# Column sums taken tile by tile, inverses nine slots behind, all constants at the start: an RWKV kernel on one core

## The chip, the cores and the metric

One core of a Trainium2 chip. The metric is the device time of one execution in microseconds (us), smaller is better; each version was run several times and its median is given. Ratios are computed as the mean time of one kernel's fast runs over that of the other's fast runs of the same rounds, so they are not quite the ratio of the medians quoted beside them. A run counts as "slow" when it is over 1.5% above the fastest of the same kernel.

## The reference, cut to what matters

```python
# k, v: (16, 2048, 256) float32; w, u: (256,)
for b in range(batch):
    aa = bb = 0; pp = -1e38                    # one state per channel
    for t in range(seq_len):
        kk, vv = k[b, t], v[b, t]
        qq = maximum(pp, u + kk); e1 = exp(pp - qq); e2 = exp(u + kk - qq)
        output[b, t] = (e1 * aa + e2 * vv) / (e1 * bb + e2 + 1e-08)
        qq = maximum(pp - w + kk, kk)           # [cut: as written]
        aa, bb, pp = e1 * aa + e2 * vv, e1 * bb + e2, qq
```

The kernel turns the loop over time into prefix sums. A tile holds 128 time steps of 4 batches (128 x 1024 values); there are 64 tiles, and four tiles (16 batches) share the same stretch of time. Between stretches, a state goes from one to the next.

## The kernel before

PE is TensorE (the matrix products), DVE VectorE, ACT ScalarE, POOL GpSimd; SP issues the small transfers. PE writes its products to PSUM, which the kernel divides into eight banks. Each turn of the loop, called a slot, brings one tile in and takes an older one out; `LAG` is how many slots behind the inverse of the denominators follows. `EZR` is a ring of twelve tiles: quarters 0 and 1 hold exponentials, quarters 2 and 3 the same times `v`.

```python
for n in range(NP + LAG + 2):                   # NP = 64, LAG = 10
    q, qp = n - LAG, n - LAG - 1
    num(qp, NUMB, 0)                            # PE: numerators, first half, into the one bank NUMB
    den(q)                                      # PE: denominators
    small_work(n, "nums")
    exps(n)                                     # ACT: exponentials of the new tile
    small_work(n, "act")
    recip(q)                                    # ACT: 1/den as Ln, then Exp
    mult(qp, NUMB, 0)                           # DVE: output, first half
    small_work(n, "mid")
    round_k(n + 2)                              # DVE: k to fp32r
    num(qp, NUMB, 1); mult(qp, NUMB, 1); store(qp)
    small_work(n, "chain")
    times_v(n)                                  # DVE: exponentials times v
    cast_v(n + 1); logs(n + 1)                  # DVE: v to bf16; PE: exponents of the next tile
    small_work(n, "pe"); small_work(n, "last")
    # [cut: the conditions for the first and last slots]
```

Once in four slots (a period) the state is worked on, spread over slots by the list `plan`. It is turned so that channels lie on partitions, worked on, turned back by PE, copied to `cb` by DVE, and sent into the tiles by four small transfers:

```python
def sums(c):                                    # PE: 32 matmuls, column sums of a period's four tiles
    ...
def inject(c):                                  # the state goes back into row 63 and 127 of four tiles
    cb = small.tile([128, 128], BF16, tag="cb", name="cb")
    K(DVE.tensor_copy(cb, st.pop((c, "CT"))))
    r0 = 4 * c % RING
    for q in range(2):                          # q = 0: the quarters that num reads; q = 1: those of den
        for h in range(2):
            r, x = HS * h + HS - 1, 32 * (2 * q + h)
            K(SP.dma_start(out=EZR[r:r + 1, 2 * (1 - q), ...], in_=cb[x:x + 32, :]))   # [cut]

plan = [(s + 1, "pe", sums), (s + 2, "mid", copy_sums), (s + 2, "pe", turn),
        (s + 3, "act", state_logs), (s + 3, "chain", state_offsets),
        (s + 4, "act", state_weights), (s + 4, "chain", state_chain),
        (s + 5, "nums", turn_back), (s + 5, "mid", inject)]      # s = 4c + 3
```

## Time and profile before

| | us |
|---|---|
| time, median of 3 runs | 331.42 (331.21 to 332.84) |
| span of the profiled run | 328.2 |
| start, to the end of the twelfth product (slot 12 begins) | 56.96 |
| middle, from there to the beginning of slot 63 | 231.66 |
| drain, from there to the end | 39.62 |

A period below is the mean of ten, slots 16 to 55. The three stages have different bounds, which is why the page's shares (PE 81%, DVE 85%, ACT 78%) decide nothing by themselves. The prediction below shows the lines: the loads and the half clock in the start, DVE in the middle, ACT's Ln and Exp pairs in the drain.

### The profile page before, as it was taken

To read this page: it belongs to the slowest core of one execution; us is meant where nothing else is said; L and a number is where in the kernel's file an instruction comes from. 1 tells how busy PE (TensorE), PEld (TensorE's weight loads), DVE (VectorE), ACT (ScalarE), POOL (GpSimd) and SP (SyncE) were. 2 spreads that over 40 slices of the span, in tenths; PEclk is the share of its full clock that TensorE was granted. 3 is DMA by queue.
4 is the path that set the end of the run, shared out by engine and by line. 5 is a ranking of instruction groups with operands and counts; after the bars stand their busy time and mean duration, and the time that the engine had idled before them with its cause. 6 is when DMAs were issued, how large, how long until landed. Compare 5 with 4: busy or idle time off the path is not lost.

```text
span 328.2 us, 4828 instructions
## 1 busy us (share of the span) xinstructions
PE 265.1 (81%) x1650; PEld 133.6 (41%) x1678; DVE 277.4 (85%) x565; ACT 256.7 (78%) x236; POOL 159.1 (48%) x207
## 2 busy tenths in 40 slices
PE   5876869888889796988888897969798867956981
PEld 2434424534444443544344444535353434523330
DVE  3979975999999989999999999899999979866453
ACT  1774539797979899797979898997979778945793
POOL 8695542464656355654646554646546411201231
PEclk9997578999999999999999999999999999978998
DMA  7999999999999999999999999999999972331666
GB/s 247 349 348 349 335 334 337 280 337 339 309 353 321 351 316 340 323 334 351 336 353 313 378 298 358 318 361 340 325 339 321 369 204 86 130 130 47 215 241 210
DMA packets 37339, 97.86 MB, mean 298 GB/s; under 512 B 6198, under 2 KB 14914, under 8 KB 37314
## 3 DMA queue, kind: packets, MB, share of 16 engines
q0 software_dynamic: 32592, 95.43, 88.6%
q1 hardware_dynamic: 4416, 1.84, 2.1%
q8 instruction: 13, 0.21, 0.3%
q10 hardware_dynamic: 306, 0.27, 0.2%
q14 instruction: 12, 0.10, 0.1%
HBM read 67.12 MB, written 33.55 MB: 307 GB/s over the span
## 4 chain that ended last, share of the span: by engine, by line
PE 44%; DVE 32%; DMA 10%; issue 4%; POOL 3%; ACT 3%; SPq 2%; DVEq 0%; POOLq 0%
PE PS L328 13%; PE PS L182 11%; PE PS L316 10%; DVE EZR L213 10%; DVE ot L334 9%; DMA EZR<-cb 7%; PE PS L177 4%; PE PS L236 4%; DVE vb L208 3%; DMA vr<-in_v_dram 3%; ACT rd L322 3%; SPq L306 2%; DVE CB L286 2%; PE PS L251 1%; DVE AB L284 1%
## 5 line engine op out<-in xcount | busy, mean ns | idle before, releaser
L195 ACT ACTIVATE EZR<-PS 128x2048 bf16<-128x2048 f32 x55 | 103.0, 1873 | 25.1 <-PE PS L182 24.9
L339 POOL DMA_DIRECT2D out_dram<-ot x63 | 48.1, 763 | 148.4 <-DVE ot L334 128.3
L334 DVE TENSOR_TENSOR ot<-PS,rd 128x512 f32<-128x512 f32 (+1 forms) x119 | 86.3, 726 | 27.9 <-PE PS L328 9.4
L213 DVE TENSOR_TENSOR EZR<-EZR,vb 128x2048 bf16<-128x2048 bf16 x64 | 77.8, 1215 | 0.0
L322 ACT ACTIVATE rd<-PS 128x1024 f32<-128x1024 f32 (+1 forms) x65 | 65.6, 1009 | 14.1 <-PE PS L316 13.9
L328 PE MATMUL PS<-EZR,LN 128*128 128x512 bf16 x126 | 48.3, 383 | 31.7 <-DVE ot L334 31.7
L323 ACT ACTIVATE rd<-rd 128x1024 f32<-128x1024 f32 (+1 forms) x65 | 68.0, 1046 | 2.1
L63 POOL DMA_DIRECT2D kr<-in_k_dram x63 | 53.7, 852 | 7.3 <-DVE km L168 3.2
L182 PE MATMUL PS<-km,NLE 128*128 128x512 f32 x128 | 48.9, 465 | 3.7 <-DVE km L168 3.7
L168 DVE CAST km<-kr 128x1024 fp32r<-128x1024 f32 x64 | 45.0, 703 | 1.1 <-DMA kr<-in_k_dram 1.0
L316 PE MATMUL PS<-EZR,L 128*128 128x512 bf16 x127 | 38.7, 386 | 8.3 <-DMA EZR<-cb 5.3
L71 POOL DMA_DIRECT2D vr<-in_v_dram x49 | 42.3, 863 | 5.2 <-DVE EZR L213 2.3
L182 PE MATMUL PS<-km,NLZ 128*128 128x512 f32 x128 | 41.8, 409 | 0.0
L328 PE MATMUL PS<-EZR,IdN 128*128 128x512 bf16 x103 | 39.5, 383 | 0.4 <-issue 0.3
L316 PE MATMUL PS<-EZR,Id 128*128 128x512 bf16 x128 | 39.0, 387 | 0.2 <-issue 0.2
L177 PE MATMUL PS<-WU,CO 32*128 32x512 f32 x256 | 36.6, 517 | 3.0 <-DVE CO L120 1.8
L208 DVE CAST vb<-vr 128x1024 bf16<-128x1024 f32 x50 | 34.6, 691 | 0.0
L328 PEld LDWEIGHTS <-IdN 128*128 128x128 bf16 x128 | 12.5, 98 | 45.5 <-issue 42.8
L193 ACT ACTIVATE EZR<-PS 128x1024 bf16<-128x1024 f32 x18 | 17.4, 1021 | 15.9 <-PE PS L182 15.9
L182 PEld LDWEIGHTS PS<-km,NLE 128*128 128x128 f32 x128 | 19.8, 195 | 20.5 <-issue 14.1
L182 PEld LDWEIGHTS PS<-km,NLZ 128*128 128x128 f32 x128 | 25.2, 197 | 6.2
L177 PEld LDWEIGHTS PS<-WU,CO 32*128 32x128 f32 x256 | 13.9, 189 | 31.5 <-issue 20.8
(59 smaller groups left out, 201.1 us busy)
## 6 DMA issues: line engine op xcount, KB each, us to landing
kr<-in_k_dram POOLq DMA_DIRECT2D x63, 512.0 KB, 8.0
out_dram<-ot POOLq DMA_DIRECT2D x63, 512.0 KB, 6.4
vr<-in_v_dram POOLq DMA_DIRECT2D x49, 512.0 KB, 8.9
vb<-in_v_dram POOLq DMA_DIRECT2D x14, 256.0 KB, 8.0
EZR<-cb SPq DMA_DIRECT2D x64, 8.0 KB, 5.3
kr<-in_k_dram SPq DMA_DIRECT2D x1, 512.0 KB, 3.9
vr<-in_v_dram SPq DMA_DIRECT2D x1, 512.0 KB, 4.8
out_dram<-ot SPq DMA_DIRECT2D x2, 128.0 KB, 2.8
```

The lines of the kernel that those rows point to most:

```text
L63: K((kq or POOL).dma_start(out=kr, in_=src[0]))
L168: K(DVE.tensor_copy(km, kr_of.pop(n)))
L177: K(PE.matmul(half(n, q)[:, i, :], CO[g:g + 32, :], WU[g:g + 32, :], start=True, stop=False, tile_position=(g, 0), skip_group_check=True))
L182: K(PE.matmul(half(n, q)[:, i, :], (NLE, NLZ)[q], km[:, i, :], start=False, stop=True, skip_group_check=True))
L195: K(SC.activation(ez(n)[:, 0:2], PS[:, 0:4, :].rearrange("p (q i) x -> p q i x", q=2), ACT.Exp))
L213: K(DVE.tensor_mul(ez(n)[:, 2:4], ez(n)[:, 0:2], vb.unsqueeze(1).broadcast_to([128, 2, 2, D])))
L316: K(PE.matmul(DENB[:, i, :], mats[m], ez(n)[:, q, i, :], start=q == 0, stop=q == 1, skip_group_check=True))
L322: K(SC.activation(rd[:, i, :], DENB[:, i, :], ACT.Ln, scale=RS))
L323: K(SC.activation(rd[:, i, :], rd[:, i, :], ACT.Exp, scale=-1.0))
L328: K(PE.matmul(bank, mats[m], ez(n)[:, q, i, :], start=q == 2, stop=q == 3, skip_group_check=True))
L334: K(DVE.tensor_mul(o[:, i, :], bank, rd[:, i, :]))
L339: K(POOL.dma_start(out=out[4 * p:4 * p + 4, c * TC:(c + 1) * TC, :].rearrange("n t d -> t n d"), in_=OT.pop(n)))
```

## The change

Its intent: take the sums of each tile as soon as it is there (8 matmuls a slot in place of 32 in a burst), follow the denominators one slot closer, make every constant before the loop instead of in slots 1 and 3, move the copy of the sums from DVE to ACT, cast `v` while PE refills the bank, and put the last state's Ln and Exp between those of the inverses.

```diff
-    LAG = 10
+    LAG = 9
     [cut: the selects for Lx and Sel go ahead of loads 1 and 3; OH, Lx, mats before the loop]
-    def sums(c):
-        for p in range(4):
-            for o in range(2): ...
+    def sums(n):
+        c, p = divmod(n, 4)
+        for o in range(2): ...                  # 8 matmuls, start only at p == 0
     def copy_sums(c):
-        K(DVE.tensor_copy(ts, st.pop((c, "tot"))))
+        K(SC.activation(ts, MISC[:, 0:Dm], ACT.Copy))
-        plan = [(s + 1, "pe", sums), (s + 2, "mid", copy_sums), (s + 2, "pe", turn), ...
-                (s + 5, "nums", turn_back), (s + 5, "mid", inject)]
+        plan = [(s + 1, "act", copy_sums), (s + 1, "pe", turn), ...
+                (s + 4, "nums", turn_back), (s + 4, "mid", inject), (s + 4, "chain", state_next)]
     [cut: the last state's logs and weights go between Ln and Exp ("recip")]
-        if out_q:
+        if q > 0 and out_q:
             den(q)
+        if 0 < n < NP:
+            sums(n - 1)
     ...
+        if n + 1 < NP:
+            cast_v(n + 1)                       # was after times_v
     ...
         if n + 1 < NP:
-            cast_v(n + 1)
             logs(n + 1)
+        if q == 0:
+            den(q)
+            recip(q)                            # the first inverse: at the end of its slot
+        if n == NP - 1:
+            sums(n)
```

Other parts that the cut leaves out: which of four tiles has its `v` cast by the load itself moves by one, `state_start` and the load of ACT's tables come later, slot 64 counts as drain already, `turn` and `turn_back` write another part of their bank than the sums, and the state's update for the next period (`state_next`) is split off.

## The prediction

> **What bounds the kernel now.** I read the page's busy slices first, then sums over stretches of time, then the chain of waits through one period, then the timeline of the start and of the drain. "Slot" below means one turn of the kernel's loop (one tile of 4 x 128 x 256 values), and four slots make a period, because the state work comes once in four slots. Slot n mod 4 is written as phase 0 to 3. A slot's start means the end of the previous product `times_v` on DVE.
>
> The sums over stretches (start:end, length, busy us and instructions of PE, PEld, DVE, ACT, POOL, then clock, DMA share, GB/s):
>
> ```profile
> 20.00:40.00 20.00, 14.77 (x86) 8.59 (x90) 18.00 (x39) 9.31 (x12) 12.59 (x19) 0.71 1.06 343
> 40.00:60.00 20.00, 15.43 (x91) 7.82 (x84) 14.48 (x31) 13.62 (x12) 6.40 (x10) 0.77 1.03 323
> 168.77:186.74 17.97, 15.42 (x107) 7.81 (x112) 16.83 (x35) 15.83 (x14) 9.90 (x13) 1.00 1.04 344
> 278.55:293.50 14.95, 10.98 (x84) 5.69 (x88) 12.41 (x28) 11.97 (x11) 3.34 (x4) 0.93 0.40 137
> 305.00:319.00 14.00, 12.45 (x53) 5.14 (x53) 7.72 (x7) 13.27 (x13) 4.53 (x6) 1.00 0.62 211
> ```
>
> Three stages show. To about 57 us: loads run at 343 to 349 GB/s with nothing idle in the DMA, and PE runs part of the time at half clock. Middle: periods of 17.97 us, DVE busy 16.83 of it (94%), ACT 15.83, PE 15.42, DMA share 1.04; everything is nearly full, so moving work from one engine to another buys little. End: from 305 us ACT is the bound, 13.27 of 14.00 us.
>
> The chain of waits in the middle (start us, length, what):
>
> ```profile
> 176.03 1.12 PE PS L182 x4
> 177.16 0.46 PE PS L328 x2
> 177.62 0.03 DVEq L334
> 177.65 0.06 DVE A L269
> 177.72 1.13 DVE EZR L213
> 178.85 0.61 DVE ot L334
> 179.46 0.04 issue
> 179.50 0.61 PE PS L328 x2
> 180.11 0.02 issue
> 180.13 0.69 DVE ot L334
> ...
> 184.59 0.59 PE PS L328 x2
> 185.19 0.44 PE PS L177 x3
> 185.62 1.12 PE PS L182 x4
> 186.74 0.32 PE PS L236 x5
> ```
>
> It alternates: half a slot's output multiply on DVE frees the one PSUM bank, PE fills it again (L328, 0.61), DVE multiplies again. No load is in the chain.
>
> A second chain nearly binds. The state goes back into the tiles by four 8 KB transfers from SP; den of the tile two slots later waits for them. Four times in the run it did:
>
> ```profile
> PE PS L316 <- DMA EZR<-cb: 5.3, 4, 2.8
> ...
> EZR<-cb SPq DMA_DIRECT2D x64, 8.0 KB, 5.3
> ```
>
> In the timeline the copy `cb` starts at 166.48 and den at 174.14, 7.66 us later. With four issues of about 0.6 us and 5.3 us to landing, the transfers need some 7.1 to 7.9 us. So there is hardly slack.
>
> **What the skill says.** "TensorE: Matmul & The Clock Gate", Part 1: after an idle window of about 3.4 us PE drops to half clock and needs a busy window to return. The trace agrees in the value (0.50 from about 30 to 42 us; the L182 pair takes 1.22 us instead of 0.73), and the drop follows a 2.8 us gap at 23.6 us, where DVE waited for POOL to make `Lx`. "ScalarE: Activation LUTs", What ACT_TABLE_LOAD costs: an activation is 186 ns plus 0.833 ns per column. The trace has 353 ns for 192 columns and 271 for 128, so the copy of 256 columns that moves to ACT should be about 0.40 us, as on DVE (414 ns). "DMA: Bandwidth & Descriptors", Issuing engines are not separate DMA queues: SP's small transfers share the 16 engines with the loads; the 5.3 us for 8 KB against 1.8 us at the shortest agrees. "PSUM — Partial Sum Buffer", The four PSUM rules: a starting matmul clears the flags of its whole bank. The new `turn_back` therefore starts no group while sums are open in the other half of the bank; no run of before shows this, it is a matter of right results.
>
> **The change part by part.**
>
> *Constants.* Before, six `Sel` selects (3.07 us of POOL at 17.2) and the `Lx` work stop loads and DVE in mid-ramp. Afterwards three `Lx` selects and two of `Sel` stand ahead of load 1: 3 x 0.33 + 2 x 0.51 = 2.0 us. Load 1 is issued at about 5.2 instead of 2.97, when load 0 has nearly drained; I put the loss of the load stream at about 0.9 us. The exp of tile 0 comes 0.6 us earlier (9.1 instead of 9.67), as the two small loads no longer follow the table load of 1.28 us. But loads arrive every 3.0 us per tile, and before, `km` of tiles 6 to 12 ran only 1.7 to 3.1 us behind arrival. So the ramp can win at most 2 to 3 us, less the 0.9. The first den waits on ACT in order (its Ln and Exp, 2.1 us, stand ahead of the next exp). Worked through slot by slot, slot 12 begins at about 56.5 instead of 57.5: **-1 us**.
>
> *Middle.* DVE loses the `ts` copy: -0.41. `sums` before was a burst, 32 matmuls, 0.99 us on the path once a period. Now it is 8 per slot. 32 take 0.99; 8 long streams of 256 columns on four column strips take about 0.21 plus the 0.13 which the burst has beyond streaming: 0.35 to 0.4 each, placed between den and the second half's num. In phases 0 and 2 that hides behind the first multiply (num starts 0.73 after it). It does not in phase 1: after `turn` (0.42) PE is late, den 0.86 and sums 0.4 lie ahead of num, and DVE, which has no cast there, waits about 0.4 for each half. In phase 3 sums must await `times_v`, then `turn_back`, so `cb` waits about 0.3. The cast moved ahead of the second multiply fills the 0.6 us in which PE refills the bank, in phases 0, 2 and 3.
>
> By phase, DVE's time from start to start, with mult 0.61 to 0.65, km 0.6, cast 0.6, times 1.15, offsets 1.37, chain 1.07: phase 0 3.6; phase 1 0.38 wait + 0.61 + 0.6 + 0.43 wait + 0.65 + 1.37 + 1.15 = 5.2; phase 2 0.61 + 0.6 + 0.6 + 0.65 + 1.07 + 1.15 = 4.7; phase 3 0.61 + 0.27 wait + 0.25 + 0.6 + 0.6 + 0.65 + 0.45 + 1.15 = 4.6. Sum 18.1. The same working applied to before gives 18.0 against the measured 17.97. If the eight sums cost 0.25 instead of 0.4, it is 17.9. So the burst is gone but its waits come back spread: **0 us**, between -5 and +4 over 13 periods.
>
> *Lag and drain.* From 305 us a slot of the drain is Ln 1.03 + Exp 1.06 + small = 2.13 us. One slot less is -2.1. Before, the last product ends at 293.1 and the last sums at 295.2 (32 matmuls at half clock behind a copy, 1.90 us); phase 3 of the last live slot carries the chain, `turn_back` and `cb` of the state before. These went a slot earlier, so the last product ends about 1.0 us earlier in its slot and sums take 0.4 to 0.8: about -2.5 together. The state's Ln and Exp (0.27 and 0.35) between the two inverses let the first Ln of the drain start without waiting; before, Ln started at 298.75, 301.07 and 305.41 before it settled to every 2.13, a loss of 2.4. Given back: the last state's transfers are sent about 14 us after the slot's start, land 4.7 later, and tile 60's den is due one slot earlier than before: about +1.1. Counted from the start of slot 63 (288.55), the end was 39.65 us away; I get 34. **-5.5 us**.
>
> Sum: -1 + 0 - 5.5 = -6.5; 331.42 - 6.5 = about 325.
>
> **Rivals.** (a) The transfers of the state become the bound. For: the gap from `cb` to den comes out as 7.4 against 7.66, with 7.1 to 7.9 needed, and den lies in the path of phase 1. Against: nothing else on SP. If each period waits 0.3 more, +4: 329. (b) PE's burst really cost its whole 0.99 and DVE at 16.4 becomes the only bound, periods near 17.4. For: DVE's sum; the cast fills idle time. Against: phases 1 and 3 above, and the DMA share of 1.04, which caps it near 6.06 MB / 349 GB/s = 17.4. That gives 13 x 0.55 = -7 more: 318. (c) The ramp goes to half clock again, since PE has only 2 us of work per 3 us; then the ramp loses 3 to 5 us: 329. (d) No half clock at all and no wait for the first state: the ramp wins 4 us more: 321.
>
> **Range and chances.** The drain is nearly certain, at least 4 us. The middle decides: 0.3 us a period is 4 us. I predict 324.5 us, 317.5 to 330 at 8 in 10. The 2% line is 324.8, so the chances are nearly even: faster 0.50, same 0.47, slower 0.03.
>
> **What would show it.** Right: periods between 17.7 and 18.2 us by the spacing of the exps; about 34 us from the last slot's start to the end; nine full Ln and Exp pairs in the drain; PE waiting for DVE less than 31.7 us in total, but DVE waiting for L316 or L328's successors in phases 1 and 3. Wrong: periods of 17.5 or less (then the burst was the bound), DMA waits of den in most periods (rival a), or a first exp of slot 12 earlier than 52 us.

## The result, and the profile after

| us | before | after |
|---|---|---|
| median (range), 4 runs each | 331.64 (331.21 to 332.84) | 328.27 (327.63 to 329.04) |
| ratio, 95% interval | | 0.989 (0.986 to 0.993) |
| span of the profiled run | 328.2 | 326.8 |
| start | 56.96 | 59.16 |
| middle | 231.66 | 231.55 |
| drain | 39.62 | 36.09 |

The time fell by 3.4 us, half of the 6.5 (or 7, from 331.42 to 324.5) predicted. The stages are of one profiled run each; these two differ by 1.4 us only (the profiled run of the kernel before took 329.95 us, less than its four timed ones), so some 2 us of the medians' difference lie in the scatter of the kernel before (326 to 336 in later rounds) and can't be put down to a stage. Nor is a stage of one profile firm: in runs 2 and 4 below, which don't touch the middle, it took 229.39 and 229.89 us, and 227.78 in run 3; and slot 12 began at 57.32 in run 1, whose program up to there differs from the changed kernel only in the order of the state's transfers.

The stretches that answer to those of before, same columns (start:end, length, busy us and instructions of PE, PEld, DVE, ACT, POOL, then clock, DMA share, GB/s); the third is one period:

```profile
20.00:40.00 20.00, 14.98 (x94) 7.56 (x94) 16.83 (x32) 11.74 (x15) 10.14 (x13) 0.83 1.06 343
40.00:60.00 20.00, 16.64 (x103) 8.26 (x105) 15.25 (x32) 15.03 (x16) 7.62 (x11) 0.92 1.03 328
153.46:171.78 18.32, 16.63 (x102) 7.68 (x104) 16.75 (x34) 16.21 (x16) 9.07 (x13) 1.00 1.03 335
305.00:319.00 14.00, 12.46 (x51) 5.11 (x51) 7.35 (x6) 12.01 (x12) 3.90 (x7) 0.96 0.62 213
```

The clock of the start is better (0.83 and 0.92 against 0.71 and 0.77), yet slot 12 begins 2.2 us later. The period is no shorter, with DVE busy 16.75 us of 18.32 (91%) where it had 94%. DVE has hardly less work: over ten periods it is busy 167.45 us instead of 168.43. The copy of the sums went (0.41 a period), but the four casts of `k` take 3.02 us instead of 2.73 (why, no run shows); the rest of the period it waits. ACT in the drain has 12.01 us where before it had 13.27: it isn't full.

**Start.** Two stretches, of before and then of after, as above:

```profile
4.00:8.00 4.00, 2.26 (x9) 0.79 (x7) 0.62 (x3) 0.00 (x0) 4.00 (x6) 1.00 1.06 356
12.00:16.00 4.00, 3.56 (x15) 1.62 (x15) 3.42 (x5) 3.63 (x4) 1.91 (x3) 1.00 1.04 351
```

```profile
4.00:8.00 4.00, 3.60 (x14) 1.19 (x12) 2.44 (x9) 0.70 (x1) 4.00 (x8) 1.00 0.86 249
12.00:16.00 4.00, 0.50 (x6) 0.13 (x5) 2.81 (x4) 1.08 (x2) 4.00 (x6) 0.58 1.02 342
```

The load stream drops from 356 to 249 GB/s in the first stretch, since the selects stand ahead of the loads on GpSimd. In the second PE is busy 0.50 of 4 us: the sums of tile 0 wait for its product, and the exponents of tile 2 stand behind them. That product is late itself: it ends at 15.45 us instead of 13.00, behind DVE's wait of 2.25 us for `k` of tile 2 and behind the cast of `v` of tile 1, which stood after it before. No run tests the cast's new place in the start alone.

**Middle.** Waits between 57 and 290 us (who waits, for whom: us, times, longest), of before and then of after:

```profile
DVE ot L334 <- issue: 8.3, 12, 0.7
DVE ot L334 <- PE PS L328: 4.1, 5, 2.0
PE PS L316 <- DMA EZR<-cb: 2.5, 3, 1.9
```

```profile
DVE ot L338 <- PE PS L332: 12.3, 13, 1.7
PEld L319 <- DMA EZR<-cb: 8.9, 9, 1.6
PE PS L319 <- DMA EZR<-cb: 3.2, 7, 0.8
DVE cb L304 <- PE PS L298: 2.7, 12, 0.2
```

L319 is den, L332 the numerators, L338 DVE's multiply, L298 the turning back, L304 its copy `cb` (before: L316 den, L328 numerators, L334 multiply; "issue" is a wait for which the profile names nobody). The wait of 0.69 us that the multiply had once a period is gone. In its place DVE now waits once a period, 0.95 us on average, for numerators that stand behind a den which waits for the state's transfers. One such place in the trace, PE and then DVE (start, length, what; in brackets the idle time before it and what ended it):

```profile
172.43 0.59 PE L319 MATMUL PS<-EZR,L 128*128 128x512 bf16 x2 [0.84 <-DMA EZR<-cb]
172.86 0.59 PE L319 MATMUL PS<-EZR,Id 128*128 128x512 bf16 x2
173.39 0.40 PE L230 MATMUL PS<-EZR,OH 128*32 128x256 bf16 x8
173.72 0.39 PE L332 MATMUL PS<-EZR,LN 128*128 128x512 bf16 x1
```

```profile
174.37 0.69 DVE L338 TENSOR_TENSOR ot<-PS,rd 128x512 f32<-128x512 f32 x1 [1.39 <-PE PS L332]
```

PE's wait of 0.84, den (0.96 with its second half), the eight sums (0.33 before the numerators start) and the numerators add up before DVE may go on: 1.39 us of idle time.

**Drain.** ACT's Ln of each tile, of before (one line) and then of after:

```profile
305.41 1.02 ACT L322 ACTIVATE rd<-PS 128x1024 f32<-128x1024 f32 x1 [2.22 <-PE PS L316]
```

```profile
296.51 1.02 ACT L325 ACTIVATE rd<-PS 128x1024 f32<-128x1024 f32 x1 [3.17 <-PE PS L319]
300.45 1.02 ACT L325 ACTIVATE rd<-PS 128x1024 f32<-128x1024 f32 x1 [1.80 <-DVE ot L338]
306.68 1.02 ACT L325 ACTIVATE rd<-PS 128x1024 f32<-128x1024 f32 x1 [4.01 <-PE PS L319]
```

After that they follow every 2.13 us, as before. ACT still loses 3.17, 1.80 and 4.01 us. The 4.01 is PE's: the trace has PE idle for 4.35 us up to the turning back of the last state (L298), which stands in program order ahead of the next numerators and denominators and waits for DVE's chain.

### The profile page after: what moved, and what is told of

It reads as the page before. It is cut to its first block, busy times and chain, and to the rows that moved or that the text cites. A ratio compares the mean times of both kernels' runs of the same rounds, so it can differ in the third digit from the quotient of the medians.

```text
span 326.8 us, 4790 instructions
## 1 busy us (share of the span) xinstructions
PE 277.6 (85%) x1649; PEld 128.6 (39%) x1678; DVE 275.7 (84%) x548; ACT 261.1 (80%) x251; POOL 149.6 (46%) x208
## 4 chain that ended last, share of the span: by engine, by line
DVE 32%; PE 31%; DMA 19%; ACT 8%; SPq 4%; issue 4%; POOL 1%; DVEq 0%; POOLq 0%; ACTq 0%
DMA EZR<-cb 11%; DVE EZR L207 10%; PE PS L176 9%; DVE ot L338 8%; DMA kr<-in_k_dram 8%; PE PS L319 8%; PE PS L332 6%; SPq L309 4%; PE PS L230 4%; ACT rd L325 3%; DVE vb L202 3%; DVE km L162 3%; PE PS L171 3%; ACT EZR L189 2%; PE PS L298 2%
## 5 line engine op out<-in xcount | busy, mean ns | idle before, releaser
L338 DVE TENSOR_TENSOR ot<-PS,rd 128x512 f32<-128x512 f32 (+1 forms) x119 | 86.0, 723 | 23.1 <-PE PS L332 12.4
L332 PE MATMUL PS<-EZR,LN 128*128 128x512 bf16 x126 | 48.5, 385 | 7.8 <-DVE ot L338 6.8
L162 DVE CAST km<-kr 128x1024 fp32r<-128x1024 f32 x64 | 47.7, 745 | 5.9 <-DMA kr<-in_k_dram 4.6
L230 PE MATMUL PS<-EZR,OH 128*32 128x256 bf16 x512 | 37.9, 286 | 16.7 <-DVE EZR L207 16.7
L61 POOL DMA_DIRECT2D kr<-in_k_dram x63 | 48.2, 766 | 8.4 <-DVE km L162 4.5
L319 PE MATMUL PS<-EZR,L 128*128 128x512 bf16 x127 | 38.3, 382 | 9.2 <-DMA EZR<-cb 3.2
L69 POOL DMA_DIRECT2D vr<-in_v_dram x49 | 38.8, 791 | 5.9 <-DVE vb L202 2.6
L332 PE MATMUL PS<-EZR,IdN 128*128 128x512 bf16 x102 | 39.1, 383 | 0.2 <-issue 0.2
L319 PE MATMUL PS<-EZR,Id 128*128 128x512 bf16 x128 | 38.2, 380 | 0.1
L202 DVE CAST vb<-vr 128x1024 bf16<-128x1024 f32 x50 | 35.7, 714 | 0.0
L171 PE MATMUL PS<-WU,CO 32*128 32x512 f32 x256 | 33.8, 509 | 2.2 <-ACT EZR L189 1.7
L230 PEld LDWEIGHTS <-OH 128*32 128x32 bf16 x512 | 12.0, 94 | 50.7 <-issue 49.5
```

The source lines that it names most:

```text
L61: K((kq or POOL).dma_start(out=kr, in_=src[0]))
L162: K(DVE.tensor_copy(km, kr_of.pop(n)))
L230: K(PE.matmul(t[32 * j:32 * j + 32, :], mats["OH"][:, x:x + 32], ez(n)[:, 2 * q, i, Dm * o:Dm * o + Dm], start=p == 0 and o == 0, stop=p = ...
L319: K(PE.matmul(DENB[:, i, :], mats[m], ez(n)[:, q, i, :], start=q == 0, stop=q == 1, skip_group_check=True))
L332: K(PE.matmul(bank, mats[m], ez(n)[:, q, i, :], start=q == 2, stop=q == 3, skip_group_check=True))
L338: K(DVE.tensor_mul(o[:, i, :], bank, rd[:, i, :]))
```

## The experiments

All ran for five rounds and all gave right results. Medians are of six runs. The first four each change one thing (with what it needs) in the changed kernel, whose own ratio to before is 0.989. That was measured in another set, and the changed kernel was not run again in these: a difference from it of under 1% is not told from a difference between the sets, and the stages are of one profiled run each.

**1. Order of the state's transfers.** Den reads the quarters that the third and fourth transfer fill; issue those first.

```diff
-        for q in range(2):
+        for q in (1, 0):
```

> The changed kernel, with the two of the four state transfers that the denominators wait for issued first instead of last; nothing else. Theory A (the state's round trip through DMA sets the middle's period of about 18.2 us): den then waits for transfers that land about 0.9 us earlier, the waits of PE for cb (3.2 us on PE and as much on its weight loads) go, and the mean period falls by 0.3 to 0.5 us; over 12 periods 3 to 6 us, so about 323 to 325 us. Theory B (the period is set by PE and DVE in turns, and the transfers only fill slack): under 1 us, about 328.

Measured: 320.23 us (319.17 to 321.86), ratio 0.969 (0.964 to 0.973). The period fell from 18.24 to 17.63, the middle from 231.55 to 224.26 (against runs 2 to 4, where these transfers are as in the changed kernel, the gain is 0.27 to 0.45 a period and 3.5 to 5.6 in the middle; their periods scatter with the transfers' landing, those of this run lie between 17.61 and 17.69). The waits for these transfers in the middle, 3.2 us on PE and 8.9 on its weight loads (the two overlap), are down to 0.4:

```profile
DVE ot L338 <- PE PS L332: 5.2, 14, 0.4
DVE cb L304 <- PE PS L298: 2.9, 13, 0.2
PEld L319 <- DMA EZR<-cb: 0.4, 1, 0.4
```

So the transfers did bound the changed kernel's middle, and the reading that nothing but DVE and PE set the period is out. DVE's remaining waits, 0.4 each, are the sums and den ahead of the numerators.

**2. Sums of the early tiles behind the logs.** The sums of tiles 0 to 6 go after `logs(n + 1)`, so that PE isn't held for the product.

```diff
-        if 0 < n < NP:
+        if EARLY <= n < NP:                     # EARLY = 8
             sums(n - 1)
     ...
             logs(n + 1)
+        if 0 < n < EARLY:
+            sums(n - 1)
     [cut: the first period's copy and turn go one place later in plan]
```

> The changed kernel, with the sums of tiles 0 to 6 put behind the logs of the next tile on PE's queue instead of ahead of them. Theory A (in the first 45 us PE stands still behind sums that await the product with v, first 3.7 us at 11.8 us, goes to half clock twice, and that costs the 3.3 us by which the ramp missed its forecast): the clock stays at 1.0 to about 35 us and slot 12 begins 2 to 3 us earlier, about 325.5 us. Theory B (the ramp is bound by the arrival of the loads, PE's order does not matter): under 0.7 us, about 328.

Measured: 325.33 us (324.14 to 328.86), ratio 0.985 (0.979 to 0.991). The exponentials of tile 2 came at 14.80 us instead of 18.03, but slot 12 began at 59.38, no earlier than 59.16. PE's gap at 12 us was real. At slot 9's exponentials 1.43 us of the gain were still there (42.06 instead of 43.49); by the first Ln they were gone, with PE at half clock up to 47.6 us in this run (0.50 from 34 to 47.6) and up to 43.3 in the changed kernel. So whether the gap at 12 us costs anything stays open. The total is 2.9 us lower than the changed kernel's, but across sets and with an interval that reaches 0.991; it proves no gain.

**3. Loads ahead of the selects.** Loads 1 to 5 are issued before any select for `Lx` and `Sel`; the matrices for the output are made in slot 1.

```diff
-    select(Lx, ...); select(Lx, ...)            # three of them
     for n in range(1, 3):
         load(n)
     ...
-    fill(Sel, 0.0); select(Sel[:, j, h], ...)   # six of them
     for n in range(3, AHEAD):
         load(n)
     ...
+    fill(Sel, 0.0); select(Sel ...); select(Lx ...)     # behind load 5
+        if n == 1:
+            out_matrices()
```

> The changed kernel, with loads 1 to 5 issued ahead of all selects of Sel and Lx, and the DVE part of the output matrices after slot 1. Theory A (the hole in the load stream at 6 to 8 us, 182 GB/s there, delays all arrivals by about 1.5 us and the ramp is bound by arrivals): DMA at 340 GB/s from 4 us on, slot 12 1 to 1.5 us earlier, about 327 us. Theory B (the ramp is bound by PE behind the sums and its half clock): under 0.5 us, about 328.

Measured: 326.29 us (321.30 to 329.46, three fast runs at 321 to 324 and three slow), ratio of the fast ones 0.977 (0.968 to 0.987). In the profiled run slot 12 began at 56.52, 2.6 us earlier. The period of this run was 17.90, the drain 37.57: other stages moved with it, so the total alone would not have told this. With runs this scattered, the 2.6 us are one profile's: run 1, with no edit to the start, began slot 12 at 57.32. All five profiles with this edit (runs 3, 5 and 10 to 12) have slot 9's exponentials at 39.37 to 40.94, earlier than all changed kernels without it (41.65 at the earliest): the direction is shown, the size isn't.

**4. Drain.** The last state's offsets and chain go behind the multiply, its turning back one slot later.

```diff
-  (s + 1, "recip", state_logs), (s + 1, "mid", state_offsets),
-  (s + 2, "recip", state_weights), (s + 2, "mid", state_chain),
-  (s + 2, "pe", turn_back), (s + 2, "last", inject)
+  (s + 1, "recip", state_logs), (s + 1, "chain", state_offsets),
+  (s + 2, "recip", state_weights), (s + 2, "chain", state_chain),
+  (s + 3, "nums", turn_back), (s + 3, "mid", inject)
```

> The changed kernel, with three things of the last state moved: its offsets and its chain after the multiply of their slot instead of before it, and turn_back and the transfers one slot later, behind the next den. Theory A (the drain missed its forecast because PE stood 4.35 us behind a turn_back that waits for the chain, and the second Ln of the drain waited 1.8 us for the rd buffer behind the offsets): the Ln of the drain come every 2.1 to 2.6 us from the first on, the drain is 3.5 to 5 us shorter, about 324 us. Theory B (the state's own chain and transfers to tile 60 set the end, whatever the order): den of tile 60 waits for cb instead, under 1.5 us gained, about 327.

Measured: 322.07 us (319.70 to 323.51), ratio 0.973 (0.968 to 0.978). The drain took 33.16 instead of 36.09, 2.93 less, where theory A had 3.5 to 5; the rest of the 6 us lies in the middle (1.66), in the start (0.47) and between the sets. PE at the turning back, and ACT's Ln:

```profile
301.00 0.40 PE L298 MATMUL PS<-Id,CB 128*128 128x128 bf16 x4 [0.73 <-DVE CB L282]
```

```profile
296.03 1.02 ACT L325 ACTIVATE rd<-PS 128x1024 f32<-128x1024 f32 x1 [4.83 <-PE PS L319]
298.18 1.02 ACT L325 ACTIVATE rd<-PS 128x1024 f32<-128x1024 f32 x1
300.31 1.02 ACT L325 ACTIVATE rd<-PS 128x1024 f32<-128x1024 f32 x1
303.17 1.02 ACT L325 ACTIVATE rd<-PS 128x1024 f32<-128x1024 f32 x1 [0.74 <-PE PS L319]
```

PE's 4.35 us became 0.73, and ACT's 1.80 and 4.01 became nothing and 0.74. The wait before the first of these Ln grew from 3.17 to 4.83: PE was at half clock there (0.57 from 292 to 296 us). Run 10 has the same edit without half clock:

```profile
280.71 1.02 ACT L313 ACTIVATE rd<-PS 128x1024 f32<-128x1024 f32 x1 [3.16 <-PE PS L307]
```

Its drain is 30.92 where run 9, without the edit, has 36.04: so there the edit is worth 5.1 us (run 10 has the loads' edit beside it, which belongs to the start).

**5. All four edits at once.**

> The four single edits at once, on the changed kernel: the two transfers that den waits for first are issued first; loads 1 to 5 stand ahead of all selects that only later work needs; the early tiles' sums stand behind the logs; the last state's offsets and chain stand behind the drain's multiply, and its turning back one slot later. Measured one at a time on the changed kernel (328.3): about -2.1%, -1.2%, -0.4% and -1.7%. Theory A (three separate causes in three separate stages: ramp, middle, drain): the gains add, so slot 12 near 56.5, periods near 17.6, drain near 33.2: 56.5 + 224.5 + 33.2 = about 314, ratio to before 0.950. Theory B (one shared bound, the load stream or DVE, over the whole run; what is won in one stage is waited for in the next): less than half of the smaller gains survives, 318 to 320, ratio 0.963 or more.

Measured: 313.99 us (313.05 to 317.05), ratio 0.957 (0.952 to 0.963). Start 56.50, period 17.79, drain 32.33. The median is theory A's, the ratio lies between the theories (0.950 and 0.963). The gains of the single stages survive together; but put down singly they add up to 5.4%, and against the changed kernel's 0.989 the ratio gives 3.2%, so the single totals of runs 1 to 4 were too good, or part of them is lost. The first two periods of the profiled run, slots 12 to 19, took 18.18 and 19.37, the later ones 17.61 to 17.63.

**6. Lag of ten alone.**

```diff
-    LAG = 9
+    LAG = 10
```

> The changed kernel with the denominators ten slots behind again and nothing else. My prediction gave one slot less of lag -2.1 us in the drain. Theory A (one slot less also takes one slot, some 4 us, out of the time that the state's transfers have, and that is where the middle lost): with ten slots PE waits for no transfer of the state, periods near 17.65 as in the run with the transfers reordered, slot 12 to slot 63 near 225 instead of 231.5, drain 2 longer, 38.2: about 323 to 324, so the lag of nine cost more than it won. Theory B (transfers don't bound the middle, the reordered run won for another reason): middle as it was, drain 2.1 longer: 330.4.

Measured: 322.18 us (321.62 to 325.28), ratio 0.984 (0.977 to 0.990), which alone can't be told from the changed kernel's 0.989. Drain 38.24, which is 2.15 longer: the prediction's 2.1 for one slot is right. Middle 224.27, which is 7.3 shorter (3.5 to 5.6 against runs 2 to 4), with no wait for a transfer: theory A, by the stages. In this kernel the slot that the lag saved in the drain was the slot that the transfers needed.

**7. The burst back.** The changed kernel with the 32 sums in the first slot of a period.

```diff
-        if 0 < n < NP:
-            sums(n - 1)
+        if 0 < n < NP and n % 4 == 0:
+            for m in range(n - 4, n):
+                sums(m)
     [cut: the same for the last period; turn_back starts its group again]
```

> The changed kernel with the sums taken as one burst of 32 matmuls in the first slot of a period again, in place of 8 in each slot; everything else as changed. My prediction: the burst comes back spread, so 0 for the middle, between -5 and +4. Theory A (prediction): period within 0.1 of the changed kernel's 18.235; only the drain's last sums grow. Total 327 to 330. Theory B (spreading won 0.5 us or more a period and the late transfers took it back): with the burst the period grows to 18.7 or more, +6 us, total 334. Theory C (spreading costs: eight sums wait for their product in each slot and stand ahead of the numerators): the period falls to 17.9 or less and slot 12 comes earlier, since no sums block the logs of the early tiles: 324 or less.

Measured: 318.07 us (316.57 to 319.08), ratio 0.968 (0.964 to 0.973). The period fell to 17.52, by 0.73 us (0.38 to 0.73 against all profiles with the changed kernel's middle): theory C, the spreading costs. The burst took 1.06 us of PE in a slot in which DVE works from product to product without a wait (3.85 us for that slot in both kernels). Spread, the sums cost in the slot with the state's copy (4.43 us spread, 4.12 as a burst): there they wait for the product and stand ahead of the turning back, so DVE waits for it, and `cb` and its transfers start later. The slot with the transfers took 5.44 spread and 5.02 with the burst.

**8. The kernel before with the transfers reordered.**

> The kernel before with the two transfers that den waits for issued first, and nothing else. Theory A (before, with a lag of ten, den comes 7.66 us after the copy, and the transfers need 7.1 to 7.9, so they bound it only now and then): gain of 0.1 to 0.2 us a period, total 329 to 331.5, class same. Theory B (the order wins for any lag, since transfers bound the middle of both kernels): periods fall by 0.5 us as in the changed kernel, total 324 to 325.

Measured: 324.39 us (323.77 to 324.91), ratio 0.988 (0.984 to 0.992). Neither theory: the period stayed (18.00 against 18.03), as A said, but the total fell, by 6 in the profiled runs and the medians and by 4 in the mean of the fast runs (five of the kernel before's eleven were slow), more than A said. It came from single places: slot 12 began at 52.91 instead of 56.96, and one late period took 18.00 instead of 19.92. In the start of the kernel before, PE stands 2.81 us (from 43.97) for the first state's transfers, and is at half clock from 45.6 to 52.4 us; reordered, it stands 1.66 us, and the clock stays whole. The same stretch of both, before and then reordered; the clock is the third number from the end:

```profile
44.00:52.00 8.00, 5.01 (x13) 2.22 (x15) 3.68 (x10) 4.28 (x5) 2.23 (x3) 0.60 1.10 330
```

```profile
44.00:52.00 8.00, 6.41 (x30) 2.98 (x32) 6.55 (x19) 6.87 (x8) 3.62 (x5) 1.00 1.11 330
```

One swapped index in the kernel before is worth as much as the whole change was (0.988 against 0.989).

The last four ran as another set, on another chip, with runs of the kernel before of their own.

**9. Order and burst** (edits 1 and 7).

> The changed kernel with two edits: the transfers that den waits for issued first, and the sums as one burst of 32 in the first slot of a period. Alone they gave periods of 17.63 and 17.52 us against 18.24. Theory A (two separate waits: the burst takes the fills in the slots 1 and 3 away from DVE, 0.3 to 0.4 us each, the order takes the transfers' wait away, 0.56 us a period as the burst's run still has it): the gains add nearly whole, period 16.9 to 17.1, total 310 to 311.5. Theory B (the load stream caps the period at my estimate of 17.4, 6.06 MB at 349 GB/s): period 17.35 to 17.5, total 315 to 317.

Measured: 316.38 us (314.19 to 317.11), ratio 0.958 (0.953 to 0.963). The period is 17.30: between the theories (the total is B's). The gains overlap (0.62 and 0.73 alone, 0.94 together), since part of what the burst won was the earlier start of the transfers. By slots it is plain: with the order set right, the slot with the transfers takes 4.82 us spread (run 1) and 4.80 with the burst, and only the slot with the state's copy differs, 4.43 and 4.12. So spreading the sums itself costs 0.3 us a period, and the rest of run 7's gain is the transfers'. It isn't the load stream: the DMA share falls from 1.04 (90 to 180 us) to 0.97 (180 to 270 us) at the same period. In one period DVE is busy 16.75 of 17.30 us, 97%:

```profile
148.23:165.53 17.30, 15.26 (x104) 7.82 (x105) 16.75 (x33) 16.01 (x16) 9.36 (x13) 1.00 1.05 357
```

**10. Order, burst, loads and drain** (edits 1, 7, 3, 4).

> As the run before it, with the two edits for the start and the drain: loads 1 to 5 ahead of the selects that only later work needs, and the last state's work behind the drain's multiply with its turning back a slot later. Theory A (gains add): another -2 in the start and -2.9 in the drain, total 306 to 308, the fastest of all. Theory B (the load stream caps the middle): 310 to 313.

Measured: 308.39 us (307.53 to 309.23), ratio 0.935 (0.932 to 0.939): start 54.72, period 17.28, drain 30.92. The two edits took 8.0 us from run 9, where theory A had 4.9; the total is still a little above its range, because run 9 lay above its own.

**11. As 10, with the first den and inverse in the usual place of their slot.**

```diff
-        if q > 0 and out_q:
+        if out_q:
             den(q)                              # and recip likewise
-        if q == 0:
-            den(q)
-            recip(q)
```

> As the run before it, with the first tile's den and inverse in the usual place of their slot (ahead of the numerators and behind that slot's exps) in place of its end, where the Ln and Exp stand ahead of the next slot's exps and hold them for the first state. Theory A (the place of the first inverse is what the start loses: exps of slot 10 wait 2.4 us behind it): slot 12 begins 1.5 to 2 earlier, total 1.5 to 2 less. Theory B (what holds the start is the first state's arrival, wherever den stands: den then blocks PE's logs instead, with half clock): same or slower, within 1 of the run before.

Measured: 306.50 us (305.95 to 307.84), ratio 0.930 (0.926 to 0.934), the fastest of all. The first Ln began at 43.92 us against 43.84 in run 10 and slot 12 at 55.08 against 54.72, so the profile shows theory B (den waits for the first state in its new place), and the times show A's 1.9 us. Its profiled run was the slowest of its six (307.84) and that of run 10 the fastest of its six (307.53). Where the 1.9 us are stays open.

**12. As 11, with a lag of ten.**

> As the run before it, with the denominators ten slots behind again. Theory A (with ten slots one more slot's exps and logs go through before the first inverse, which waits for the first state anyway, so the start gains what the drain loses: slot 12 about 53 to 54, as in the kernel before with reordered transfers, drain +2.1): total within 1.5 of the runs before it, so the lag is worth about nothing. Theory B (lag nine is a gain once the transfers are out of the way): start unchanged, total 2 more than the run before it.

Measured: 309.75 us (307.89 to 311.08), ratio 0.939 (0.935 to 0.943). Start 52.63, which is 2.45 earlier; drain 33.06, which is 2.13 longer; period 17.40 against 17.28. Of the 2.45, 1.25 lie ahead of slot 9's exponentials, where the two programs don't differ yet. Of the theories, A has the stages and B the total: with the transfers out of the way the lag of nine is a gain, 1% in the times.

**What sets the start.** Put side by side, the traces show what none of my theories had. The starts of slot 9's exponentials, of the first Ln and of slot 12, us:

| run | lag | exponentials of slot 9 | first Ln | slot 12 | from the Ln to slot 12 |
|---|---|---|---|---|---|
| after | 9 | 43.49 | 47.96 | 59.16 | 11.20 |
| 1, order | 9 | 41.65 | 46.13 | 57.32 | 11.19 |
| 2, early sums | 9 | 42.06 | 48.18 | 59.38 | 11.20 |
| 3, loads | 9 | 40.84 | 45.31 | 56.52 | 11.21 |
| 4, drain | 9 | 43.03 | 47.50 | 58.69 | 11.19 |
| 5, four edits | 9 | 40.82 | 45.29 | 56.50 | 11.21 |
| 7, burst | 9 | 42.53 | 47.00 | 57.90 | 10.90 |
| 9, order and burst | 9 | 42.57 | 47.04 | 57.92 | 10.88 |
| 10, with loads and drain | 9 | 39.37 | 43.84 | 54.72 | 10.88 |
| 11, first den in its usual place | 9 | 40.94 | 43.92 | 55.08 | 11.16 |
| before | 10 | 39.77 | 48.70 | 56.96 | 8.26 |
| 6, lag 10 | 10 | 42.77 | 50.84 | 57.26 | 6.42 |
| 8, before reordered | 10 | 39.41 | 46.12 | 52.91 | 6.79 |
| 12, as 11 with lag 10 | 10 | 39.69 | 45.67 | 52.63 | 6.96 |

From the first Ln on, ACT goes from one instruction to the next (Ln 1.0, Exp 1.1, exponentials 1.9, about 4.0 us a slot), so slot 12 follows at a fixed distance, and with a lag of nine one slot more lies after that point: 11.16 in run 11, 6.96 in run 12, which differ in the lag alone. The first Ln comes 3.0 us sooner after slot 9's exponentials for it, so the lag's net cost in the start is 1.2 us: from slot 9's exponentials to slot 12 it is 14.14 against 12.94 in these two, and 15.67 against 14.49 in the changed kernel and run 6. In the changed kernel the first den stands at the end of slot 9, behind the exponents of tile 10, and these wait for the banks that slot 9's exponentials free; so the first Ln comes 4.47 us after the start of those exponentials (4.48 once) in all the kernels of lag nine that place it there, but for run 2. ACT, of after:

```profile
43.49 1.88 ACT L189 ACTIVATE EZR<-PS 128x2048 bf16<-128x2048 f32 x1 [2.29 <-PE PS L176]
...
47.96 1.02 ACT L325 ACTIVATE rd<-PS 128x1024 f32<-128x1024 f32 x1 [2.43 <-PE PS L319]
49.02 1.06 ACT L327 ACTIVATE rd<-rd 128x1024 f32<-128x1024 f32 x1
49.98 1.86 ACT L189 ACTIVATE EZR<-PS 128x2048 bf16<-128x2048 f32 x1
```

So the start splits in two: slot 9's exponentials are late, and the first inverse stands ahead of one slot more. How late they are goes with the clock, in the profiles at hand. Runs 1, 4 and 6 have the changed kernel's program up to there, but for the order of the transfers in run 1, and start them at 41.65, 43.03 and 42.77 instead of 43.49; in the same order the mean clock from 30 to 44 us was 0.88, 0.63, 0.76 and 0.63. The changed kernel, then run 1 (columns as above):

```profile
30.00:44.00 14.00, 10.73 (x62) 5.66 (x61) 11.09 (x21) 5.95 (x9) 6.73 (x9) 0.63 1.07 339
30.00:44.00 14.00, 9.35 (x68) 4.97 (x65) 11.84 (x25) 7.93 (x10) 7.76 (x10) 0.88 1.08 339
```

So of the 3.7 us by which they are later than before, 1.8 are missing in run 1, with no edit to the start. At one clock, 0.76, run 3 (loads) has 40.84, runs 7 and 9 (burst) 42.53 and 42.57, run 6 (neither) 42.77: 1.9 us for the loads' edit and 0.2, which is nothing, for the burst. This was read from the traces after the runs; the lag's part is tested by runs 11 and 12 and by run 6, the rest is observation.

## Why the prediction was right or wrong

**Its range held; its size did not.** 324.5 was predicted, 328.3 measured: a gain half as large, and within 2% where more than 2% had been held slightly likelier.

**Constants and start: -1 predicted, +2.2 measured (+0.4 to +2.2 in the profiles of runs 1 and 4 and the changed kernel, whose start is the same). This step failed.** The working took the loads' arrival, every 3.0 us, as the bound of the start, and gave the first inverse only its own 2.1 us. The loss of the load stream was there (249 GB/s; load 1 was issued at 4.75 us, sooner than the 5.2 forecast, since the two `Sel` selects took 0.23 us each and not 0.51), and was worth some 1.9 us at slot 9 rather than 0.9 (run 3 against run 6; single profiles). Slot 9's exponentials came 3.7 us later than before, 1.9 in run 1. And the lag counts in the start too, 1.2 us net (runs 6, 11 and 12), which the working counted in the drain alone. That the sum is only +2.2 is because the kernel before lost time there that the changed one didn't lose: it waited for the first state and went to half clock (run 8 wins 4.05 us there). Rival (c), half clock again, was seen as well: 0.58 in 12 to 16 us, where run 2 leaves open what it cost, and 0.50 from 33.1 to 43.3 us. Run 1 was at half clock there only up to 35.4 us and began slot 12 at 57.32: 1.8 of the 2.2 us go with the clock, as far as single profiles tell.

**Middle: 0 predicted, -0.1 measured, for other reasons than those given.** The hand sum of 18.1 us against 18.24 looks good, and DVE's waits of 1.08 a period against (12.3 + 2.7) / 13 = 1.15 too. But phase 1, worked out at 5.2 without a transfer, takes 4.82 where no transfer is waited for (run 1) and 5.44 where one is; and DVE's busy time fell by 0.10 a period, not by the 0.41 of the copy. But the zero was a sum of parts that the working didn't have. The burst, put at 0.99 us on the path, costs nothing in the slot where run 7 has it. Spreading it was a loss (0.3, run 9 against run 1). The transfers' wait, set aside as rival (a), was there (0.62 by run 1, 0.27 to 0.62 by all profiles); the prediction's own sign of it, waits of den for DMA in most periods, came true with 7 on PE and 9 on its weight loads in some 13 periods. Without both, the same kernel's period is 17.30 (run 9): the rest of the change, the earlier cast, the copy on ACT and the rearranged state, was worth about 0.7 us a period against the 18.03 of before (these were not tested one by one), and the two costs took it back. The prediction had written down that a gap of 7.4 us stood against a need of 7.1 to 7.9, and still let it cost nothing in the central number. Run 6 shows that the slot saved in the lag is the one that was missing.

The size of the eight sums was right: 0.35 to 0.4 predicted, 0.40 measured. So was the copy on ACT: 0.40 predicted, 0.38 to 0.39 measured, which agrees with the formula of the Trainium skill, "ScalarE: Activation LUTs", What ACT_TABLE_LOAD costs.

**Lag and drain: -5.5 predicted, -3.5 measured. The term for ACT's waits failed.** One slot of lag was 2.15 (run 6) as predicted. (The terms that the working lists add up to -5.9; it wrote -5.5.) But the state's Ln and Exp between the inverses did not free ACT: the first Ln of the drain waited 3.17 us, and the next two 1.80 and 4.01 (2.22 in the same place before). The working followed ACT only. In the trace PE takes its matrix products in program order, and the turning back ahead of the numerators held PE for 4.35 us, and so the denominators that ACT needed. Run 4 takes that wait away and gives 2.9 us back, with PE at half clock ahead of the first Ln: 33.16, against the 34 predicted; run 10 has 30.92 at full clock.

## What to carry to other kernels

Before a distance is shortened, list what travels over it: one slot less of lag won 2.15 us at the end, cost 1.2 in the start and up to 7.3 in the middle, there because a small transfer used that slot. Ask of several transfers which one is waited for first, and issue it first. And where work is spread to shorten a burst, look whether the burst stood in a place where the critical engine had work anyway; each of the spread pieces gets a place in an in-order queue, ahead of something.

## What the Trainium skill lacked or had wrong

- "DMA: Bandwidth & Descriptors": it has figures for the first byte and for the fixed cost of a transfer, and none for how long a small transfer takes beside a full load stream. Here an 8 KB transfer between buffers took 1.8 us from issue to landing when no load was left (kernel before, issued at 293.3 us), and 5.3 to 5.5 us in the median of the run. Two transfers issued first instead of last, some 1.2 us earlier, were worth 3.5 to 7.3 us over the middle (run 1).
- "TensorE: Matmul & The Clock Gate", Part 1: half clock comes after at least one idle window of about 3.4 us. Here gaps of 3.71 and 4.35 us went with half clock, but so did one of 2.81 us (kernel before, from 43.97; half clock from 45.6). A gap of 2.09 us was followed by half clock in run 4 (the next numerators took 0.63 us) and by full clock in the changed kernel (0.38 us). The moments at which the clock changes lie a multiple of 3.41 us apart (changed kernel: 12.61, 19.44, 33.09, 43.33 us by the trace's clock records), which agrees with the page's free-running window; but the gaps of 2.09 and 2.81 us are shorter than one window. The limit of about 3 us in the page's section "Why this matters for your kernels" was not a safe one here.
